# A hybrid decoder block on one core: norm 2's sums in halves, and five precomputed pieces placed differently around norm 2

## The chip, the core and the metric

The kernel runs on one core of one Trainium2 chip. The metric is the device time of one execution in microseconds (us). Before the change it took 804.24 us, the median of 3 runs (802.44 to 804.77).

## What is computed

One layer on 512 tokens of width 1024, all in float32. The reference, cut to what matters:

```python
h = rmsnorm(x, norm1_g)
z = h @ w_in + b_in
z_glu, z_rx, z_rg, z_ga, z_gb = split(z)
u   = silu(layernorm(causal_conv(glu(z_glu))))          # 31 taps
y_a = u @ conv_w_out + conv_b_out
y_b = (rg_lru(causal_conv(z_rx)) * gelu(z_rg)) @ lru_w_out
m = sigmoid(z_ga) * y_a + sigmoid(z_gb) * y_b
x = x + m @ w_mix_out
h = rmsnorm(x, norm2_g)                                  # "norm 2"
x = x + (silu(h @ ffn_w1) * (h @ ffn_w3)) @ ffn_w2       # d_ff = 2816
return rmsnorm(x, norm_f_g)
```

## The kernel before

**Products.** Each float32 operand is split into a high part (rounded to the matmul's format) and a low part (the rest), and a product is three matmuls: high by high, high by low, low by high. A weight chunk (512 KB) is loaded by SyncE into one of 4 `raw` buffers, ScalarE casts its high part (`split_to`, line 128), and VectorE (GpSimd in the first part of the kernel) subtracts for the low part (line 124) into one of 5 `hl` buffers. `emit_chunk` does this; the chunks have a fixed order and are asked for a few ahead.

**Seven products instead of eight.** Three large products (w_mix_out, most of ffn_w1/ffn_w3, ffn_w2) are cut into 2 x 2 blocks and made with seven block products, which needs sums of blocks on both sides. On the weights' side, the sums of ffn_w1, ffn_w3 and ffn_w2 are made piece by piece: `piece_load` brings two halves of 256 KB into one of 3 `wsums` buffers, `piece_sums` does four operations of 128 x 256 on GpSimd or VectorE (lines 124 and 375), and `piece_store` writes the 512 KB result to DRAM (line 379), from where it is later loaded as a chunk (`raw_ft`, `raw_ot`). Most pieces are made on GpSimd early in the kernel. The last four of ffn_w1/ffn_w3 and the first of ffn_w2 (`fwso` in the trace) are made around norm 2 by `mix_end`; the other pieces of ffn_w2 follow on VectorE in `out_step`.

**Around norm 2.** `mix_end` finishes the product with w_mix_out. Tokens are handled in two halves of 256 (tiles 0, 1 and tiles 2, 3). For each half the row sums of squares are made by ScalarE (lines 514 and 520), the rows scaled by VectorE (`xs`, line 1056), transposed by TensorE (line 538), and split into `h2h`, `h2l` by ScalarE and VectorE (lines 541 and 542). TensorE, ScalarE and VectorE follow the written order there. While the second half is prepared, TensorE multiplies the first half with the first four weight chunks f1_0, f3_0, f1_1, f3_1 (line 498); then it does the second half of these, the chunks f1_2 to f3_3 with all tokens, and from then on pairs of tiles by seven products (`ffn_seven`, line 1189), beginning with pair 2. Pair k uses the chunks fb11, fb20, fb21 (straight from the weights), ft00, ft01, ft10, ft11 (from the stored sums).

**On the activations' side** of `ffn_seven`, `f_inputs` needs the sum h2h + h2l of all eight row blocks: before, GpSimd makes these as eight operations of 128 x 512 (`hf`, line 1148) once norm 2 is wholly done. VectorE then makes four sums of 128 x 256 for each of four pairs (`hs`) and splits them (`hs_0h`, `hs_0l`, `hs_1h`, `hs_1l`).

**What orders the work.** Outside the written stretches a scheduler places the instructions; `tc.issue_after(x)` keeps an instruction behind instruction x. All transfers but a few stand in SyncE's queue, which issues them in its order: a transfer that waits (for a buffer or for a sum to be stored) holds all behind it. GpSimd, VectorE and ScalarE also run in order.

Of the kernel before, what the change touches and what calls it, by code (L numbers as in the profile page):

```python
# [8 lines left out]
F32 = mybir.dt.float32  # L9
F32R = mybir.dt.float32r  # L10
AF = mybir.ActivationFunctionType
ALU = mybir.AluOpType
# [14 lines left out]
ND = D // P  # L27
# [26 lines left out]
F_MIX, OUT_MIX, LATE_LAG = 4, 1, 8  # L54
# [37 lines left out]
def tile_block(ctx, tc, a, out):  # L92
    nc = tc.nc
# [8 lines left out]
    def tiles(tag, bufs):  # L102
        p_ = pool(tag, bufs)
        return lambda name, dtype=F32: p_.tile([P, T], dtype, tag=tag, name=name)

    longt, shortt = tiles("long", SLOTS), tiles("short", SHORT)

    def pairt(name, dtype=F32R):

        return longt(f"{name}h", dtype), longt(f"{name}l", dtype)  # L110
# [7 lines left out]
    vec, act, pe, pool_e = nc.vector, nc.scalar, nc.tensor, nc.gpsimd  # L118


    newest = {}

    def sub(eng, o, x, y):
        return eng.tensor_tensor(out=o, in0=x, in1=y, op=ALU.subtract)  # L124
# [9 lines left out]
    def split(name, full, eng, p_=None, copy=act.copy):  # L134
        p_ = p_ or pairt(name)
        return split_to(*p_, full, eng, copy)
# [40 lines left out]
    def emit_to(n):  # L177
        while emitted[0] < min(len(chunks), n):
            emit_chunk()
# [170 lines left out]
    def f_piece(k, i, c):  # L350

        four = (w1, w3)[i].rearrange("p (h k) n -> p h k n", h=2)
        halves = [four[:, h, c : c + 2, 2 * k * P : 2 * (k + 1) * P] for h in range(2)]
        return f"{k}_{i}_{c}", halves, f_sums[k][:, i, :, c * 256 : c * 256 + T]

    def o_piece(k, c):
        four = outq.w.rearrange("p (k h) (e n) -> p h k e n", h=2, e=2)
        cs = slice(256 * c, 256 * c + 256)
        return f"o{k}_{c}", [four[:, h, k, :, cs] for h in range(2)], outq.all_sums[k][:, :, cs]

    def piece_load(name, halves):
        raw = wsums.tile([P, 1024], F32, tag="wsum", name=f"fws{name}")
        for h, src in enumerate(halves):
            nc.sync.dma_start(raw[:, h * T : h * T + T].rearrange("p (e n) -> p e n", e=2), src)
        return raw

    def piece_sums(raw, dest, eng):
        if dest.shape[1] == 2:
            of = raw.rearrange("p (h k e n) -> p h e k n", h=2, k=2, e=2)
        else:  # L370
            of = raw.rearrange("p (h e n) -> p h e n", h=2, e=2)
        q11, q12, q21, q22 = (of[:, h, e] for h in range(2) for e in range(2))
        sub(eng, q22, q22, q12)
        sub(eng, q12, q12, q11)
        eng.tensor_tensor(out=q11, in0=q22, in1=q11, op=ALU.add)  # L375
        sub(eng, q21, q21, q11)

    def piece_store(raw, dest):
        nc.sync.dma_start(dest, raw.rearrange("p (m n) -> p m n", m=dest.shape[1]))
# [43 lines left out]
    x2_kept = [[dram.tile([P, T], F32, tag=f"x2k{t}{h}", name=f"x2k{t}{h}") for h in range(2)] for t in range(NT)]  # L423
# [8 lines left out]
    for name, n in ROWS:  # L432
# [4 lines left out]
        while done < n:  # L437
            m = min(n - done, P - row_at(at + done)[1])
# [70 lines left out]
    def rstd_begin(half, junk):  # L509

        i = n_stats[0]
        n_stats[0] += 1
        ss, r = stats[:, i, :2], stats[:, i, 2:3]
        act.activation(junk, half, AF.Square, accum_out=ss[:, 0:1])
        vec.tensor_scalar(out=ss[:, 0:1], in0=ss[:, 0:1], scalar1=1.0 / D, scalar2=EPS, op0=ALU.mult, op1=ALU.add)
        return ss, r

    def rstd_end(begun, half, junk):
        ss, r = begun
        act.activation(junk, half, AF.Square, accum_out=ss[:, 1:2])  # L520
        act.activation(r, ss[:, 1:2], AF.Sqrt, scale=1.0 / D, bias=ss[:, 0:1])
        vec.reciprocal(r, r)
        return r
# [222 lines left out]
    behind = [None, None]  # L746
# [114 lines left out]
    f_todo = [f_piece(k, i, c) for k in SEVEN for i in range(2) for c in (0, 2)]  # L861
    out_todo = [o_piece(k, c) for k in range(KF) for c in range(2)]
# [37 lines left out]
    LO, HI = HALVES  # L900
# [124 lines left out]
    x2 = [[longt(f"x2{t}{h}") for h in range(2)] for t in range(NT)]  # L1025
# [3 lines left out]
    h2p = [pairt(f"h2{c}") for c in range(ND)]  # L1029
    xs = []  # L1030

    def mix_end(second, plus, r1, r2, r7, third):
        todo = f_todo[-F_MIX:] + [out_todo.pop(0) for _ in range(OUT_MIX)]
        made = []

        def begin(behind=None):

            name, halves, dest = todo.pop(0)
            with tc.issue_after(behind or newest["any"]):
                made.append((piece_load(name, halves), dest))  # L1040
            piece_sums(*made[-1], pool_e)

        def store(behind=None):
            with tc.issue_after(behind or newest["any"]):
                piece_store(*made.pop(0))

        for _ in range(2):
            begin()
        sc = [[longt(f"xs{t}{h}") for h in range(2)] for t in range(NT)]
        xs.extend(sc)  # L1050
        begun = [rstd_begin(x2[t][0], sc[t][0]) for t in range(2)]

        def scaled(t, h):
            r = rstd_end(begun[t], x2[t][h], sc[t][h])
            for i in range(2):
                vec.tensor_scalar(out=sc[t][i], in0=x2[t][i], scalar1=r, scalar2=None, op0=ALU.mult)
                newest["kept"] = nc.sync.dma_start(x2_kept[t][i][:, :], x2[t][i]).ins


        with tc.manual_schedule(engines={ET.PE, ET.Activation, ET.DVE}):  # L1060
            second()
            plus(0, 1, r1[0])
            plus(0, 1, r2[0])
            plus(2, 1, r1[0])
            plus(1, 1, r1[1])
            plus(1, 1, r2[1])
            plus(3, 1, r1[1])
            for t in range(2):
                scaled(t, 1)
            begin(newest["kept"])  # L1070
            store(newest["kept"])

            for i in range(2):
                third(i, range(2))
            for q in range(2):
                turn_half("th", xs, "norm2_g", h2p, 0, [bank, bank2], range(4 * q, 4 * q + 4))
                for i in range(2):
                    third(i, [2 + q])
            begin()
            store()  # L1080
            for i in range(2):
                plus(2 + i, 1, r7[i])
                plus(2 + i, 0, r7[i])
            begun.extend(rstd_begin(x2[t][1], sc[t][1]) for t in (2, 3))
            emit_to(emitted[0] + 1)
            begin()
            for i in range(2):
                plus(2 + i, 0, r1[i])
            for t in (2, 3):
                scaled(t, 0)  # L1090
        while made:
            store()
        assert not todo

    m7.run(x2, lambda k: None, mix_end)


# [3 lines left out]
    def out_step(k):  # L1101


        if out_at[1]:
            with tc.issue_after(newest["any"]):
                piece_store(*out_at[1])
        if out_at[0]:
            with tc.issue_after(newest["now"]):
                piece_sums(*out_at[0], vec)
        out_at[1], out_at[0] = out_at[0], None  # L1110
        if out_quota.get(k, 0):
            out_quota[k] -= 1
            name, halves, dest = out_todo.pop(0)
            with tc.issue_after(newest["any"]):
                out_at[0] = piece_load(name, halves), dest
# [27 lines left out]

    def f_inputs():
        for k in range(4):
            a1, a2 = [longt(f"hf{c}") for c in (k, k + 4)]
            for v, c in ((a1, k), (a2, k + 4)):
                pool_e.tensor_tensor(out=v, in0=h2p[c][0].bitcast(F32), in1=h2p[c][1].bitcast(F32), op=ALU.add)
            g = [longt(f"hs{k}_{i}") for i in range(2)]
            s1, s2, s3, s4 = (v[:, cs] for v in g for cs in HALVES)  # L1150
            add(s1, a1[:, HI], a2[:, HI])
            sub(vec, s2, s1, a1[:, LO])
            sub(vec, s3, a1[:, LO], a1[:, HI])
            sub(vec, s4, a2[:, LO], s2)
            s12, s34 = [split(f"hs{k}_{i}", v, vec) for i, v in enumerate(g)]
            for n, p_, cs in (
                ("a11", h2p[k], LO), ("a12", h2p[k + 4], LO), ("a22", h2p[k + 4], HI),
                ("s1", s12, LO), ("s2", s12, HI), ("s3", s34, LO), ("s4", s34, HI),
            ):
                f_in[n].append(tuple(v[:, cs] for v in p_))  # L1160

    with tc.issue_after(turned):
        f_inputs()


    WHERE = {
# [80 lines left out]
    x2 = [[longt(f"x2b{t}{h}") for h in range(2)] for t in range(NT)]  # L1247
# [99 lines left out]
```

## Time and profile before

| | us |
|---|---|
| median of 3 runs | 804.24 |
| the profiled execution | 804.67 |
| its span, first to last instruction | 802.9 |
| TensorE busy | 791.2 |
| VectorE busy | 689.3 |
| ScalarE busy | 465.1 |
| GpSimd busy | 282.2 |

The mean TensorE clock granted is 0.999 of full speed. In the profile PE is TensorE (PEld its weight loads), DVE is VectorE, ACT is ScalarE, POOL is GpSimd and SPq is SyncE's queue. A row of a timeline gives the start and the duration in us, the engine, the line, the operation, output <- inputs, the shape, and in brackets the idle time before it and what ended that. Several equal operations in a row are merged (xN) and their joint duration given. Buffer numbers are left out of names, so that all `hl_f` chunks, for example, share one name; which is which follows from their order.

### The profile page before, as it was taken

What the parts mean: (1) busy time and instruction counts of PE and PEld (TensorE: products, weight loads), DVE (VectorE), ACT (ScalarE), POOL (GpSimd) and SP (SyncE); (2) the same over time, 40 slices, a digit from 0 to 9 for tenths busy, and PEclk for the clock granted to TensorE, in tenths of its full rate; (3) what the DMA queues carried; (4) which work ended last, traced back from release to release, by engine and by line L of the source; (5) the groups of instructions that cost most, each with busy time, mean ns of one, the idle gap of its engine ahead of it and who ended that gap; (6) DMA issues with size and microseconds to landing.
All of it is one profiled execution on the core that took longest, in us unless ns stands there. A gap on an engine that the chain in (4) does not pass through costs nothing.

```text
span 802.9 us, 12487 instructions
## 1 busy us (share of the span) xinstructions
PE 791.2 (99%) x4398; PEld 692.7 (86%) x4398; DVE 689.3 (86%) x1092; ACT 465.1 (58%) x666; POOL 282.2 (35%) x239
## 2 busy tenths in 40 slices
PE   8999999999999999999999999999999999999996
PEld 8988888888888888888888898899999999988885
DVE  5799999998999997776898868977778778999956
ACT  7446788766589655653336454444445445656753
POOL 2576678756878976112230365000000000000000
PEclk9999999999999999999999999999999999999999
DMA  7646565666676775578979768599889889878652
GB/s 221 188 125 178 164 193 168 205 198 175 196 215 207 238 242 160 171 238 268 301 250 306 233 217 262 159 312 298 288 287 302 275 283 305 272 225 282 202 171 105
DMA packets 188561, 182.35 MB, mean 227 GB/s; under 512 B 13671, under 2 KB 153363, under 8 KB 188499
## 3 DMA queue, kind: packets, MB, share of 16 engines
q1 hardware_dynamic: 188355, 181.30, 72.3%
q8 instruction: 34, 0.56, 0.3%
q14 instruction: 28, 0.23, 0.1%
q10 hardware_dynamic: 144, 0.26, 0.1%
HBM read 141.81 MB, written 36.70 MB: 222 GB/s over the span
## 4 chain that ended last, share of the span: by engine, by line
PE 85%; DVE 6%; DMA 5%; ACT 2%; issue 1%; SPq 1%; ACTq 0%; DVEq 0%
PE z L498 35%; PE fr L1189 15%; PE or L950 13%; PE yb L498 7%; PE ya L498 5%; PE mxr L950 5%; DMA raw_fb<-in_ffn_w_dram 3%; PE g L819 3%; PE f L498 2%; DVE hl_fb L124 1%; ACT hl_fb L128 1%; DVE fwso L124 1%; DMA raw_f<-in_ffn_w_dram 1%; DMA x<-in_x_dram 1%; DMA ot<-fwso 1%
## 5 line engine op out<-in xcount | busy, mean ns | idle before, releaser
L692 DVE SCALAR_TENSOR_TENSOR cv<-u,par,cv 128x511 f32<-128x511 f32 (+17 forms) x240 | 162.7, 728 | 1.1 <-ACT cv L689 0.9
L124 POOL TENSOR_TENSOR hl_in<-raw_in,hl_in 128x1024 fp32r<-128x1024 f32 x51 | 123.2, 2421 | 70.0 <-ACT hl_in L128 56.9
L124 POOL TENSOR_TENSOR fws<-fws 128x256 f32<-128x256 f32 x108 | 90.1, 838 | 125.8 <-DMA fws<-in_ffn_w_dram 120.9
L124 DVE TENSOR_TENSOR hl_fb<-raw_fb,hl_fb 128x1024 fp32r<-128x1024 f32 x27 | 34.1, 1263 | 29.1 <-ACT hl_fb L128 28.9
L1189 PE MATMUL fr<-hs_0h,hl_ft 128*128 128x256 f32 x288 | 53.8, 285 | 2.4 <-DVE hl_ft L124 1.6
L128 ACT CAST hl_in<-raw_in 128x1024 fp32r<-128x1024 f32 x51 | 53.1, 1042 | 1.1 <-issue 1.0
L128 ACT CAST hl_fb<-raw_fb 128x1024 fp32r<-128x1024 f32 x27 | 28.3, 1049 | 39.2 <-DMA raw_fb<-in_ffn_w_dram 34.0
L1189 PEld LDWEIGHTS fr<-hs_0h,hl_ft 128*128 128x128 f32 x288 | 45.5, 192 | 3.4 <-DVE hl_ft L124 1.8
L124 DVE TENSOR_TENSOR hl_ft<-raw_ft,hl_ft 128x1024 fp32r<-128x1024 f32 x36 | 43.8, 1218 | 4.7 <-ACT hl_ft L128 4.7
L498 PE MATMUL z<-h10h,hl_in 128*128 128x512 f32 (+1 forms) x110 | 41.4, 378 | 0.0
L498 PE MATMUL z<-h11h,hl_in 128*128 128x512 f32 (+1 forms) x110 | 41.1, 376 | 0.0
L498 PE MATMUL z<-h16h,hl_in 128*128 128x512 f32 (+1 forms) x110 | 41.1, 376 | 0.0
L498 PE MATMUL z<-h14h,hl_in 128*128 128x512 f32 (+1 forms) x110 | 41.1, 376 | 0.0
L498 PE MATMUL z<-h17h,hl_in 128*128 128x512 f32 (+1 forms) x110 | 41.1, 375 | 0.0
L498 PE MATMUL z<-h15h,hl_in 128*128 128x512 f32 (+1 forms) x110 | 41.1, 375 | 0.0
L498 PE MATMUL z<-h13h,hl_in 128*128 128x512 f32 (+1 forms) x110 | 41.1, 375 | 0.0
L498 PE MATMUL z<-h12h,hl_in 128*128 128x512 f32 (+1 forms) x110 | 41.1, 375 | 0.0
L1189 PE MATMUL fr<-hs_0l,hl_ft 128*128 128x256 f32 x144 | 40.7, 283 | 0.0
L1197 ACT ACTIVATE c<-c 128x256 f32<-128x256 f32 x27 | 11.3, 418 | 47.5 <-DVE c L899 47.4
L128 ACT CAST hl_ft<-raw_ft 128x1024 fp32r<-128x1024 f32 x36 | 36.8, 1042 | 2.8 <-DMA raw_ft<-fs 2.8
L128 ACT CAST hl_ob<-raw_ob 128x1024 fp32r<-128x1024 f32 (+1 forms) x23 | 23.4, 1016 | 21.3 <-PE or L950 13.4
L375 POOL TENSOR_TENSOR fws<-fws 128x256 f32<-128x256 f32 x36 | 28.9, 806 | 2.5
(940 smaller groups left out, 2618.5 us busy)
## 6 DMA issues: line engine op xcount, KB each, us to landing
raw_in<-in_w_in_dram SPq DMA_DIRECT2D x52, 512.0 KB
fws<-in_ffn_w_dram SPq DMA_DIRECT2D x72, 256.0 KB
fs<-fws SPq DMA_DIRECT2D x36, 512.0 KB
raw_ft<-fs SPq DMA_DIRECT2D x36, 512.0 KB
fwso<-in_ffn_w_dram SPq DMA_DIRECT2D x44, 256.0 KB
ot<-fwso SPq DMA_DIRECT2D x22, 512.0 KB
raw_fb<-in_ffn_w_dram SPq DMA_DIRECT2D x18, 512.0 KB
raw_ob<-in_ffn_w_dram SPq DMA_DIRECT2D x33, 256.0 KB
```

The lines of the kernel that those rows point to most:

```text
L124: return eng.tensor_tensor(out=o, in0=x, in1=y, op=ALU.subtract)
L128: copy(h, full)
L375: eng.tensor_tensor(out=q11, in0=q22, in1=q11, op=ALU.add)
L498: pe.matmul(ps, l, r, start=i == 0, stop=i == n - 1)
L692: vec.scalar_tensor_tensor(out=acc[c][:, s:], in0=u[c][:, : T - s], scalar=dw(c, s), in1=acc[c][:, s:], op0=ALU.mult, op1=ALU.add)
L819: pe.matmul(ps, l, r, start=k == 0, stop=k == len(mms) - 1)
L950: pe.matmul(banks[i], l_[:, ts], r_, start=start and n == 0, stop=stop and n == 2, skip_group_check=again)
L1189: pe.matmul(ps[:, HALVES[i]], lw[:, c, :], rx_, start=not (again or i or c or m), stop=bool(i and c == 3 and m == 2), skip_group_check=True,)
L1197: act.activation(c[:, LO], c[:, LO], AF.Silu)
```

## The change

1. GpSimd's eight sums `hf` of 512 columns become sixteen of 256 columns. Those of the first half of tokens (LO) stand in `mix_end`, behind the first half of norm 2; those of the second half (HI) stay in `f_inputs`.
2. Of the five pieces around norm 2, the first three are loaded ahead together. The sums of two are made at once as before, those of the third behind the first halves (LO). The fourth and fifth are loaded behind norm 2's written stretch, and their sums stand behind the second halves (HI), in turns in the program's order.
3. The stores of the first three pieces stand at the end of `mix_end`, behind the newest load there; those of the fourth and fifth are given out by `out_step`, one each time that it is called, behind the newest load.

```diff
+    mix_made = []
+    mix_todo = f_todo[-F_MIX:] + [out_todo.pop(0) for _ in range(OUT_MIX)]
+    f_full = []
+    def full(dst, c, cs):
+        newest["full"] = pool_e.tensor_tensor(out=dst, in0=h2p[c][0][:, cs].bitcast(F32), in1=h2p[c][1][:, cs].bitcast(F32), op=ALU.add).ins
...
-        for _ in range(2):
-            begin()
+        for n in range(3):
+            name, halves, dest = mix_todo.pop(0)
+            with tc.issue_after(newest["any"]):
+                made.append((piece_load(name, halves), dest))
+            if n < 2:
+                piece_sums(*made[-1], pool_e)
...
-            begin(newest["kept"])
-            store(newest["kept"])
...
-            begin()
-            store()
+            for c in range(ND):
+                f_full.append(longt(f"hf{c}"))
+                full(f_full[c][:, LO], c, LO)
+            with tc.issue_after(newest["full"]):
+                piece_sums(*made[2], pool_e)
...
-            begin()
...
+        if mix_made:
+            with tc.issue_after(newest["any"]):
+                piece_store(*mix_made.pop(0))
...
-            a1, a2 = [longt(f"hf{c}") for c in (k, k + 4)]
-            for v, c in ((a1, k), (a2, k + 4)):
-                pool_e.tensor_tensor(out=v, in0=h2p[c][0].bitcast(F32), in1=h2p[c][1].bitcast(F32), op=ALU.add)
+            a1, a2 = f_full[k], f_full[k + 4]
+            full(a1[:, HI], k, HI)
+            full(a2[:, HI], k + 4, HI)
...
+    with tc.issue_after(newest["any"]):
+        for name, halves, dest in mix_todo:
+            mix_made.append((piece_load(name, halves), dest))
     with tc.issue_after(turned):
         f_inputs()
+    for m in mix_made:
+        with tc.issue_after(newest["full"]):
+            piece_sums(*m, pool_e)
```

In the program that results, TensorE's instructions stand in the same order as before. In SyncE's queue the stores of the first two pieces now stand ahead of the load of chunk f1_2, and the third piece's store ahead of the load of f3_3. Then come the load of fb11, the fourth piece's store, the load of a piece of ffn_w2, the load of fb20, the fifth piece's store, the load of another piece, and the load of fb21.

More of the change, by code (lines that the diff above doesn't have):

```diff
@@ L1030, in tile_block, with store @@
     xs = []
+    mix_made = []
[3 more added lines that the diff above has]
+        newest["full"] = pool_e.tensor_tensor(out=dst, in0=h2p[c][0][:, cs].bitcast(F32), in1=h2p[c][1][:, cs].bitcast(F32), op=ALU.add).ins
     def mix_end(second, plus, r1, r2, r7, third):
-        todo = f_todo[-F_MIX:] + [out_todo.pop(0) for _ in range(OUT_MIX)]
         made = []
-        def begin(behind=None):
-            name, halves, dest = todo.pop(0)
-            with tc.issue_after(behind or newest["any"]):
-                made.append((piece_load(name, halves), dest))
[L1041 to L1045, printed above, removed]
-        for _ in range(2):
-            begin()
+        def store():
+            with tc.issue_after(newest["any"]):
+                piece_store(*made.pop(0))
+        for n in range(3):
+            name, halves, dest = mix_todo.pop(0)
+            with tc.issue_after(newest["any"]):
+                made.append((piece_load(name, halves), dest))
+            if n < 2:
+                piece_sums(*made[-1], pool_e)
         sc = [[longt(f"xs{t}{h}") for h in range(2)] for t in range(NT)]
@@ L1056, in scaled @@
                 vec.tensor_scalar(out=sc[t][i], in0=x2[t][i], scalar1=r, scalar2=None, op0=ALU.mult)
-                newest["kept"] = nc.sync.dma_start(x2_kept[t][i][:, :], x2[t][i]).ins
+                nc.sync.dma_start(x2_kept[t][i][:, :], x2[t][i])
         with tc.manual_schedule(engines={ET.PE, ET.Activation, ET.DVE}):
@@ L1092, in mix_end @@
             store()
-        assert not todo
     m7.run(x2, lambda k: None, mix_end)
@@ L1160, in f_inputs @@
                 f_in[n].append(tuple(v[:, cs] for v in p_))
+    with tc.issue_after(newest["any"]):
+        for name, halves, dest in mix_todo:
+            mix_made.append((piece_load(name, halves), dest))
     with tc.issue_after(turned):
         f_inputs()
+    for m in mix_made:
+        with tc.issue_after(newest["full"]):
+            piece_sums(*m, pool_e)
     WHERE = {
```

## The prediction

> **What bounds the kernel now.** I read the page first, then the waits of TensorE, the matmuls around the one long wait, and the engine in front of it. Part 1 of the page:
>
> ```profile
> PE 791.2 (99%) x4398; PEld 692.7 (86%) x4398; DVE 689.3 (86%) x1092; ACT 465.1 (58%) x666; POOL 282.2 (35%) x239
> ```
>
> TensorE is busy for 791.2 of 802.9 us, and the diff gives it the same matmuls in the same order. So the change can only act where TensorE waits. All its waits behind norm 2 (us in total, times, longest):
>
> ```profile
> PE fr L1189 <- DVE hl_ft L124: 1.6, 1, 1.6
> ...
> PE fr L1189 <- ACT c L1203: 0.6, 2, 0.3
> PE f L498 <- ACT h20h L541: 0.3, 1, 0.3
> ```
>
> The third is the turn of the second half of tokens (transpose, ScalarE, matmul); nothing in it is edited. The first two make 2.2 us: the most that the change can give, since it touches nothing else that TensorE waits for. The rows of TensorE in time (start, duration) place the long one:
>
> ```profile
> 470.12 0.60 PE L538 MATMUL th<-ident,xs 128*128 128x128 f32 x4
> ...
> 484.65 0.40 PE L498 MATMUL f<-h20l,hl_f 128*128 128x512 f32 x1
> ...
> 516.40 0.28 PE L1189 MATMUL fr<-hs_0l,hl_ft 128*128 128x256 f32 x1
> 518.25 0.50 PE L1189 MATMUL fr<-hs_0h,hl_ft 128*128 128x256 f32 x2 [1.57 <-DVE hl_ft L124]
> ```
>
> At 516.40 TensorE needs the low part of chunk ft01 of pair 2. VectorE makes it in program order, and these are its rows:
>
> ```profile
> 467.09 1.65 DVE L1056 TENSOR_SCALAR xs<-x,stats 128x512 f32<-128x512 f32 x2
> ...
> 476.32 0.48 DVE L542 SCALAR_TENSOR_TENSOR h27l<-th,par,h27h 128x256 fp32r<-128x256 f32 x1
> 476.72 1.41 DVE L124 TENSOR_TENSOR hl_f<-raw_f,hl_f 128x1024 fp32r<-128x1024 f32 x1
> 478.49 1.88 DVE L124 TENSOR_TENSOR hl_f<-raw_f,hl_f 128x1024 fp32r<-128x1024 f32 x1 [0.36 <-ACT hl_f L128]
> ...
> 481.34 1.28 DVE L124 TENSOR_TENSOR hl_f<-raw_f,hl_f 128x1024 fp32r<-128x1024 f32 x1 [0.18 <-ACT hl_f L128]
> 485.74 1.62 DVE L124 TENSOR_TENSOR hl_f<-raw_f,hl_f 128x1024 fp32r<-128x1024 f32 x1 [3.13 <-ACT hl_f L128]
> 487.28 0.41 DVE L1122 TENSOR_TENSOR ou<-si,f 128x256 f32<-128x256 f32 x1
> ...
> 488.72 2.31 DVE L124 TENSOR_TENSOR hl_fb<-raw_fb,hl_fb 128x1024 fp32r<-128x1024 f32 x1
> 490.95 1.77 DVE L124 TENSOR_TENSOR ous0l<-ou,ous0h 128x512 fp32r<-128x512 f32 x1
> ...
> 497.44 0.68 DVE L124 TENSOR_TENSOR hs_1l<-hs,hs_1h 128x512 fp32r<-128x512 f32 x1
> ...
> 500.76 1.22 DVE L124 TENSOR_TENSOR hl_fb<-raw_fb,hl_fb 128x1024 fp32r<-128x1024 f32 x1 [0.25 <-ACT hl_fb L128]
> ...
> 516.98 2.35 DVE L124 TENSOR_TENSOR hl_ft<-raw_ft,hl_ft 128x1024 fp32r<-128x1024 f32 x2
> ```
>
> VectorE reaches the wanted split only at 516.98, done near 518.1. Between 485.74 and 516.98 it hardly pauses, so its backlog is set at 485.74. Two things made it: a pause of 3.13 us before 485.74, and two splits that took 2.31 and 1.77 us where an equal shape takes 1.22 (500.76) and 0.68 (497.44). For the pause I follow ScalarE, SyncE's queue and the chain of waits:
>
> ```profile
> 461.40 1.98 ACT L128 CAST hl_f<-raw_f 128x1024 fp32r<-128x1024 f32 x2
> 464.33 0.63 ACT L520 ACTIVATE xs<-x 128x512 f32<-128x512 f32 x1 [0.94 <-DVE x L899]
> ...
> 484.66 1.05 ACT L128 CAST hl_f<-raw_f 128x1024 fp32r<-128x1024 f32 x1 [1.97 <-DMA raw_f<-in_ffn_w_dram]
> ```
>
> ```profile
> 453.30 0.42 SPq L153 DMA_DIRECT2D raw_f<-in_ffn_w_dram  x1
> ...
> 468.48 0.37 SPq L379 DMA_DIRECT2D fs<-fws  x1
> ...
> 477.08 0.60 SPq L379 DMA_DIRECT2D ot<-fwso  x1
> 477.74 1.61 SPq L1057 DMA_DIRECT2D x2k<-x  x2
> 479.39 0.65 SPq L153 DMA_DIRECT2D raw_f<-in_ffn_w_dram  x1
> ...
> 481.75 1.59 SPq L364 DMA_DIRECT2D fwso<-in_ffn_w_dram  x2
> 483.44 0.55 SPq L153 DMA_DIRECT2D raw_fb<-in_ffn_w_dram  x1
> ```
>
> ```profile
> 479.39 5.24 DMA raw_f<-in_ffn_w_dram
> ...
> 518.12 4.48 DMA ot<-fwso
> ...
> 562.90 7.03 DMA raw_fb<-in_ffn_w_dram
> ```
>
> The load of chunk f3_3 stood in SyncE's queue behind the store of the fifth piece (477.08), which waited for GpSimd. It was issued at 479.39, took 5.24 us, and ScalarE cast it at 484.66. GpSimd's rows:
>
> ```profile
> 447.02 1.82 POOL L375 TENSOR_TENSOR fws<-fws 128x256 f32<-128x256 f32 x1
> ...
> 452.08 0.74 POOL L124 TENSOR_TENSOR fws<-fws 128x256 f32<-128x256 f32 x1
> 464.96 1.74 POOL L124 TENSOR_TENSOR fws<-fws 128x256 f32<-128x256 f32 x2 [12.15 <-DMA fws<-in_ffn_w_dram]
> ...
> 477.01 2.28 POOL L1148 TENSOR_TENSOR hf<-h20h,h20l 128x512 f32<-128x512 f32 x1
> ...
> 483.73 1.29 POOL L1148 TENSOR_TENSOR hf<-h25h,h25l 128x512 f32<-128x512 f32 x1
> ```
>
> A sum over 256 columns takes 0.74 us, or 1.82 beside a large split of VectorE; one over 512 takes 1.29, or 2.28. So a blocked sum loses about 1.0 to 1.1 us.
>
> **The change part by part.**
>
> *First halves.* Eight sums of 256 columns follow norm 2's first half, 8 x 0.74 = 5.9 us, inside the 12.15 us that GpSimd idled before 464.96: hidden. The third piece is loaded with the first two, so its four sums follow at once, 4 x 0.74 plus one block of 1.08: done near 466. No engine waits there that waited for nothing before, except SyncE (second rival). If that cover went, GpSimd would reach the second halves later, and VectorE asks for those only behind the split of 490.95.
>
> *The load of f3_3* now has the third piece's store ahead of it: issued near 466 instead of 479.39. The 3.13 us pause goes. What is late next is TensorE: VectorE's product ou needs the first two tiles, whose last matmul ends where the next tile starts, 484.65, say 485.0 with its tail. Before, ou stood at 487.28: **2.3 us won** on VectorE.
>
> *Second halves and the two late pieces.* The second halves follow h27l (476.32 + 0.48); with a last one blocked by the split of 476.72, GpSimd is free near 478.9. Then come eight sums, of pieces four and five in turn; piece four is whole after the seventh. Seven x 0.74 = 5.2 us, plus three blocks of 1.08 by the splits like those of 478.49, 481.34 and 485.74, gives 487.3. Bounds: no block at all and the halves done at 477.5, 482.7; every sum at 1.82, 490.2 from 477.5 and 491.6 from 478.9. I take 487.3, because a block needs an overlap and there are three large splits. GpSimd then leaves VectorE alone from about 488 instead of 492, so the 1.09 + 1.09 us excess of the two splits mostly goes.
>
> By the Trainium skill, page "SBUF — State Buffer", section "SBUF: two separate sides", GpSimd and a VectorE instruction with two SBUF inputs take one port pair by an exclusive lock, and the other "fully blocks". The rows agree: 2.31 against 1.22 us, 1.82 against 0.74. By that rule alone every small VectorE sum would be a possible block as well, and piece four would be whole between 487.3 and the upper bound; it speaks against moving sums into this stretch.
>
> *SyncE's queue* is the price. Behind piece four's store now stand, in order, the loads of an output piece (1.59 us) and of chunk fb20, then the store of piece five, loads of the next output piece (which wait for piece four's buffer) and fb21. So fb20 is issued at 487.3 + 0.4 + 1.6 = 489.3, not at 483.44. It lands 5.24 us later, 494.5 (4.48 to 7.03 in the chain's rows: 493.8 to 496.3); cast 1.05, split 1.22, then hs_1l 0.68: 497.4. Before, VectorE ended hs_1l near 498.1. With everything loaded, VectorE would have been there at 498.1 - 2.3 - 2.2 = 493.6. So **the late load gives back 3.8 of 4.5 us**, and 0.7 to 0.8 are left. Chunk fb21: piece four's store lands 4.48 after 487.3, two loads of 1.6, so it is issued at 493.4, lands 498.6, is split by 501 at the latest; before, that split ended at 502.0. It adds nothing.
>
> *The rest of VectorE's queue* to ft01 holds the same instructions in a slightly other order, with GpSimd silent in both kernels: it moves by the same 0.8. The split ends at 517.3 instead of 518.1, and of the 1.57 us wait about 0.8 stays. The two waits for c (0.6 together) follow loads that themselves moved by 0.8, as TensorE did: they stay.
>
> *Sum.* 1.57 - 0.8 = 0.8 us saved. The profiled execution took 804.67 us for a span of 802.9; it lies 0.4 above the median of 804.24. From the median: 804.24 - 0.8 = **803.4 us**.
>
> **The rivals.**
>
> *The gain is whole.* If GpSimd is hardly blocked (piece four at 482.7 to 486), fb20 lands 1.3 to 4.6 us sooner, VectorE is at least 2.1 us ahead, and the 1.57 go, with up to 0.6 of the waits for c: 2.2 us, **802.0**. For it speaks that 464.96 shows 0.87 a sum beside VectorE; against it, that five large splits fall into 476.7 to 488.
>
> *The new wait takes all (the other side).* Mechanism: SyncE stands before piece four's store, and VectorE waits for fb20. It decides at 487.3 + 0.8 = 488.1: every microsecond that GpSimd ends later lengthens TensorE's wait by the same. At 491.6, every sum blocked, ft01 is done 3.5 us later than before: **807.7**. For it: 477.01, where sums ran at 2.28 in a row; against: VectorE has no pieces that dense between 480 and 485.
>
> *No net change.* GpSimd at about 488, or one landing 0.8 us slower (7.03 stands in the chain): **804.2**, a new wait in the place of the old.
>
> *Norm 2 itself late.* The load of f1_2 now queues behind the stores of the first two pieces, whose sums end at 452.08 + 0.74, and one copy of x2: issued near 454, where the load of 453.30 stood. ScalarE casts it in the pair at 461.40, ahead of the squares of 464.33. VectorE ends xs at 468.74 and TensorE wants it at 470.12: 1.4 us of slack. A landing after 464.7, 10.7 us after issue against 7.03 at most above, would cost one for one; at 467, 2.3 us: **806.5**. Unlikely.
>
> That the change doesn't do what it says can be left out: the moved sums stand so in the program.
>
> **How the numbers follow.** Forecast (0.2 to 1.4 saved, 802.8 to 804.0) 0.40; whole gain 0.20; no net change 0.16; late fb20 0.18; norm 2 late 0.06. Runs of before spread over 802.44 to 804.77, so about 0.3%, 2.4 us, is what a measurement can tell from no change. Faster than 801.8 needs the whole gain and luck: 0.10. Slower than 806.65 needs the outer half of the two slow cases: 0.12. Within: 0.78. Range: 801.4 (whole gain and 0.6 of spread) to 806.6 (where at most one in ten is above).
>
> **What would show it.** Right: VectorE's pause before the fourth hl_f split gone, and a pause of two to four us before the second hl_fb instead, behind a load that SyncE issued right behind piece four's store near 487; TensorE's wait for hl_ft near 0.8. Wrong: GpSimd's eight late sums done before 485 and no pause at that split (whole gain), or ended after 489 with a longer wait for hl_ft; ScalarE's squares of the second half waiting for a cast.

## The result, and the profile after

The changed kernel takes 805.76 us (median of 22 runs, 804.79 to 808.77), the kernel before 804.12 us (22 runs in turns with it, 801.47 to 806.07). The ratio is 1.0025, with a 95% interval of 1.0016 to 1.0035: **slower** by 1.6 us by the medians and 2.0 by the ratio, where 0.8 us faster was forecast.

The profiled execution of after took 804.81 us, span 802.7 us, which is near the fastest of its runs; that of before took 804.67, which is above its median. So these two profiles, set side by side, show almost no difference; three more of each kernel stand below. TensorE's waits behind norm 2 in after (us in total, times, longest):

```profile
PE fr L1203 <- ACT c L1217: 1.3, 2, 1.0
PE fr L1203 <- DVE hl_ft L124: 1.2, 1, 1.2
...
PE f L498 <- ACT h20h L541: 0.3, 1, 0.3
```

The wait for chunk ft01 (hl_ft) went from 1.57 to 1.23, not to 0.8, and the waits for c (ScalarE's copy of a finished block product, which has to be made before TensorE adds the next product to it) went from 0.6 to 1.3. TensorE's rows in time, each wait with the matmul ahead of it and the one behind it where they are used below:

```profile
470.90 0.97 PE L498 MATMUL f<-h20h,hl_f 128*128 128x256 f32 x5 [0.35 <-ACT h20h L541]
...
514.56 0.28 PE L1203 MATMUL fr<-hs_1h,hl_fb 128*128 128x256 f32 x1
515.15 0.39 PE L1203 MATMUL fr<-hs_0h,hl_ft 128*128 128x256 f32 x1 [0.31 <-ACT c L1217]
515.37 0.28 PE L1203 MATMUL fr<-hs_0l,hl_ft 128*128 128x256 f32 x1
...
518.31 0.50 PE L1203 MATMUL fr<-hs_0h,hl_ft 128*128 128x256 f32 x2 [1.23 <-DVE hl_ft L124]
...
538.03 0.39 PE L1203 MATMUL fr<-hs_0h,hl_ft 128*128 128x256 f32 x1 [0.99 <-ACT c L1217]
```

VectorE's rows that answer to those of before (start, duration):

```profile
483.49 1.73 DVE L124 TENSOR_TENSOR hl_f<-raw_f,hl_f 128x1024 fp32r<-128x1024 f32 x1 [0.65 <-ACT hl_f L128]
485.15 0.41 DVE L1130 TENSOR_TENSOR ou<-si,f 128x256 f32<-128x256 f32 x1
...
491.70 0.68 DVE L124 TENSOR_TENSOR hs_0l<-hs,hs_0h 128x512 fp32r<-128x512 f32 x1
496.36 1.23 DVE L124 TENSOR_TENSOR hl_fb<-raw_fb,hl_fb 128x1024 fp32r<-128x1024 f32 x1 [3.98 <-ACT hl_fb L128]
497.50 0.68 DVE L124 TENSOR_TENSOR hs_1l<-hs,hs_1h 128x512 fp32r<-128x512 f32 x1
...
517.04 2.35 DVE L124 TENSOR_TENSOR hl_ft<-raw_ft,hl_ft 128x1024 fp32r<-128x1024 f32 x2
```

The old pause (3.13 us before 485.74) is gone, and ou stands at 485.15 where 485.0 was forecast. A new pause of 3.98 us stands before the split of fb20, where two to four were forecast. Yet hs_1l ends at 498.18, not at 497.4: that is where it ended before, and from there VectorE runs as late as before (517.04 against 516.98). GpSimd's seventh late sum, which makes piece four whole, SyncE's queue and ScalarE's cast of fb20 show the chain:

```profile
485.79 0.75 POOL L124 TENSOR_TENSOR fws<-fws 128x256 f32<-128x256 f32 x1
```

```profile
465.55 0.42 SPq L153 DMA_DIRECT2D raw_f<-in_ffn_w_dram  x1
...
478.14 0.93 SPq L339 DMA_DIRECT2D raw_fb<-in_ffn_w_dram  x2
486.56 0.37 SPq L379 DMA_DIRECT2D fs<-fws  x1
487.02 1.35 SPq L364 DMA_DIRECT2D fwso<-in_ffn_w_dram  x2
488.46 0.60 SPq L153 DMA_DIRECT2D raw_fb<-in_ffn_w_dram  x1
489.15 0.60 SPq L379 DMA_DIRECT2D ot<-fwso  x1
489.84 1.70 SPq L364 DMA_DIRECT2D fwso<-in_ffn_w_dram  x2
491.63 1.49 SPq L153 DMA_DIRECT2D raw_fb<-in_ffn_w_dram  x1
```

```profile
495.28 1.05 ACT L128 CAST hl_fb<-raw_fb 128x1024 fp32r<-128x1024 f32 x1 [3.85 <-DMA raw_fb<-in_ffn_w_dram]
```

Piece four is whole at 486.54 (forecast 487.3) and SyncE stands from 479.07 to 486.56 before its store. The load of fb20, issued at 488.46, lands at 495.28: 6.8 us, not 5.24. The stretches of the DMA queue show what it left with (length, clock, busy share of the 16 DMA engines, GB/s):

```profile
484.00:488.00 4.00, 1.00 0.14 52
488.00:490.00 2.00, 1.00 0.89 263
...
492.00:494.00 2.00, 1.00 1.06 365
494.00:496.00 2.00, 1.00 1.08 380
```

While SyncE waited, the DMA engines were all but idle; then two stores, four loads of pieces and fb21 came out together with fb20 and shared the engines with it. In the other three executions of after the same load took 7.0, 6.3 and 6.9 us. That the crowd stretched it is argued from these rows and not tested: before, f3_3's 5.24 us fell into engines that were about as busy (0.84 to 1.07 between 478 and 484).

### The profile page after: what moved, and what is told of

It reads as the page before. It is cut to its first block, busy times and chain, and to the rows that moved or that the text cites. A ratio compares the mean times of both kernels' runs of the same rounds, so it can differ in the third digit from the quotient of the medians.

```text
span 802.7 us, 12502 instructions
## 1 busy us (share of the span) xinstructions
PE 791.2 (99%) x4398; PEld 692.9 (86%) x4398; DVE 686.9 (86%) x1092; ACT 465.1 (58%) x666; POOL 281.6 (35%) x247
## 4 chain that ended last, share of the span: by engine, by line
PE 88%; DVE 5%; DMA 3%; ACT 1%; issue 1%; SPq 0%; DVEq 0%; ACTq 0%
PE z L498 35%; PE fr L1203 17%; PE or L950 13%; PE yb L498 7%; PE ya L498 5%; PE mxr L950 5%; PE g L819 3%; PE f L498 3%; DMA raw_fb<-in_ffn_w_dram 1%; DMA ot<-fwso 1%; DVE fwso L124 1%; DVE hl_ft L124 1%; DVE hl_fb L124 1%; DMA x<-in_x_dram 1%; PE th L538 0%
```

## The experiments

The theory: the load of fb20, held in SyncE's queue behind GpSimd's late sums, eats VectorE's lead. The rivals: that ScalarE's and VectorE's new order behind pair 2 costs by itself; that GpSimd's sums cost through the port that they share with VectorE; that the difference is noise of the kernel's start.

One table for all. "Split" is the start of VectorE's split of ft01, counted from the row of TensorE's first matmul behind the second turn (470.90 in after, the first row above); "behind" is the time from that row to the end of the span. In the kernel with the sums ahead (E2), where TensorE waits for nothing there, it wants ft01 45.45 us behind that row; a split needs 1.27 us from its start to the waiting matmul (517.04 to 518.31), so the split must start by 44.2.

| kernel | median us (runs) | ratio to before, 95% | split | behind |
|---|---|---|---|---|
| before, four profiles | 804.12 (22) | | 45.9, 44.3, 45.3, 46.2 | 331.8, 330.1, 331.3, 331.7 |
| after, four profiles | 805.76 (22) | 1.0025 (1.0016 to 1.0035) | 46.1, 46.4, 45.6, 46.2 | 331.8, 332.6, 331.7, 332.5 |
| E2 sums ahead | 801.15 (12) | 0.9973 (0.9958 to 0.9988) | 40.8 | 328.2 |
| E3 halves alone | 801.11 (12) | 0.9970 (0.9956 to 0.9985) | 41.9 | 328.2 |
| E4 pieces alone | 807.63 (7) | 1.0053 (1.0031 to 1.0074) | 42.8 | 333.9 |
| E6 stores later | 802.30 (12) | 0.9979 (0.9964 to 0.9993) | 42.2 | 329.2 |
| E7 in turn | 802.93 (12) | 0.9984 (0.9973 to 0.9995) | 42.7 | 330.0 |
| E8 load early | 804.15 (12) | 0.9997 (0.9985 to 1.0008) | 45.1 | 331.6 |

The medians follow the last column: from E2 to the mean of before (331.2) it grows by 3.0, and so do they.

**E1, the changed kernel again.**

> The changed kernel again, unedited, for a second profile. First theory (the held load): the profile shows VectorE's pause of 3 to 5 us ahead of the second hl_fb split and TensorE's wait for hl_ft at 0.8 to 2 us again, 804.8 to 807. Rival (the gain is there, and something unrelated, such as the start of the kernel or the clock, moves the time from run to run): the waits behind norm 2 differ by over 1 us between the two profiles, or the time differs where these waits are the same.

Measured: 805.79 us (12 runs), ratio 1.0024 (1.0008 to 1.0040). The wait for hl_ft is 1.22 and VectorE's pause 4.19; the waits for c are 1.7. The first theory's line held. TensorE's waits at the start differ between the two profiles (2.0 us against 0.5), but its row behind the second turn comes only 0.2 us later; 0.8 of the 1.0 us between the two spans lies behind that row, where the waits for c are longer.

**E2, the late sums ahead of the second halves.** Only GpSimd's order changes.

```diff
...
     with tc.issue_after(newest["any"]):
         for name, halves, dest in mix_todo:
             mix_made.append((piece_load(name, halves), dest))
-    with tc.issue_after(turned):
-        f_inputs()
     for m in mix_made:
-        with tc.issue_after(newest["full"]):
+        with tc.issue_after(newest["sums"]):
             piece_sums(*m, pool_e)
+    with tc.issue_after(turned):
+        f_inputs()
```

> The changed kernel with one thing moved: GpSimd makes the sums of pieces four and five ahead of the second halves (HI) and not behind them, so that their stores hold nothing up in SyncE's queue. All other engines keep the order of the changed kernel. First theory (the held load of fb20 is what eats the lead): fb20's load is issued near 481 to 484, not 488.5, VectorE's pause ahead of its split goes, TensorE's wait for hl_ft at 518 goes from 1.2 to 0, and the time falls by 1.2 to 2.2 us, to about 803.7 at the median, below the kernel before or equal to it. Rival (VectorE's and ScalarE's order behind pair 2, the same in both, makes the waits): the time stays within 0.5 us of the changed kernel, with 2 us or more of waits behind norm 2. Second rival (GpSimd and VectorE share a port, and the sums now meet norm 2's second half): TensorE waits for h2 near 470 to 480 and the time rises.

Measured: 801.15 us, by the medians 4.6 below the changed kernel and 2.9 below the kernel before, more than was expected. Behind norm 2 TensorE's only wait is the turn. SyncE issues fb20 at 481.33, the DMA engines are busy at 1.04 from 480 to 484, where the share was 0.35 in after, and VectorE has no pause ahead of fb20's split and, behind GpSimd's last sum, no stretched one (SyncE, a stretch, GpSimd's last sum, VectorE):

```profile
481.33 0.62 SPq L153 DMA_DIRECT2D raw_fb<-in_ffn_w_dram  x1
```

```profile
480.00:484.00 4.00, 1.00 1.04 318
```

```profile
478.50 1.72 POOL L1038 TENSOR_TENSOR hf<-h27h,h27l 128x256 f32<-128x256 f32 x1
```

```profile
483.42 1.23 DVE L124 TENSOR_TENSOR hl_f<-raw_f,hl_f 128x1024 fp32r<-128x1024 f32 x1 [1.09 <-ACT hl_f L128]
...
511.63 2.35 DVE L124 TENSOR_TENSOR hl_ft<-raw_ft,hl_ft 128x1024 fp32r<-128x1024 f32 x2
```

The split of ft01 starts 5.4 us sooner. The order of VectorE and ScalarE is the changed kernel's (as it is in E3, E6 and E7), and its waits for c are gone too: the order alone costs nothing. What this run leaves open is which of the two, the queue or the port, did it, since the late sums are out of VectorE's way as well.

**E3, the halves alone**, in the kernel before; the five pieces stay, only the third piece's sums stand behind the first halves.

```diff
...
-            begin(newest["kept"])
+            begin(newest["kept"], False)
+            third_piece = made[-1]
...
+            for c in range(ND):
+                f_full.append(longt(f"hf{c}"))
+                full(f_full[c][:, LO], c, LO)
+            with tc.issue_after(newest["full"]):
+                piece_sums(*third_piece, pool_e)
             begin()
...
-            for v, c in ((a1, k), (a2, k + 4)):
-                pool_e.tensor_tensor(out=v, in0=h2p[c][0].bitcast(F32), in1=h2p[c][1].bitcast(F32), op=ALU.add)
+            full(a1[:, HI], k, HI)
+            full(a2[:, HI], k + 4, HI)
```

> The kernel before with part one of the change alone: norm 2's sums in halves of tokens, the first halves at once; the five pieces' loads and stores stay where they were, with the third piece's sums behind the first halves. First theory: no load behind norm 2 is held longer than before, f3_3's load still waits for the stores (the 3 us pause of VectorE stays), the second halves are done 5 us sooner than the whole sums were, and the time is that of the kernel before within 0.8 us, 803.3 to 804.5. Rival (the halves themselves cost, by more operations on the shared port): 805 to 806, as the changed kernel.

Measured: 801.11 us. Neither line held: it was expected to change nothing, and it takes 3.0 us off the median. GpSimd is done at 485.45, not at 492, and leaves VectorE alone from there:

```profile
484.71 0.74 POOL L1035 TENSOR_TENSOR hf<-h27h,h27l 128x256 f32<-128x256 f32 x1
```

```profile
487.57 1.22 DVE L124 TENSOR_TENSOR hl_fb<-raw_fb,hl_fb 128x1024 fp32r<-128x1024 f32 x1
488.70 0.69 DVE L124 TENSOR_TENSOR ous0l<-ou,ous0h 128x512 fp32r<-128x512 f32 x1
```

Before, the last two took 2.31 and 1.77. Of the change's parts it is the early half of the sums that pays, and TensorE waits for nothing more behind the turn: the waits for c are gone with the one at ft01.

**E4, the pieces alone**: the changed kernel with whole sums behind norm 2, and the third piece's sums made at once.

```diff
-            if n < 2:
-                piece_sums(*made[-1], pool_e)
+            piece_sums(*made[-1], pool_e)
...
-            for c in range(ND):
-                f_full.append(longt(f"hf{c}"))
-                full(f_full[c][:, LO], c, LO)
-            with tc.issue_after(newest["full"]):
-                piece_sums(*made[2], pool_e)
...
-            full(a1[:, HI], k, HI)
-            full(a2[:, HI], k + 4, HI)
+            for v, c in ((a1, k), (a2, k + 4)):
+                newest["full"] = pool_e.tensor_tensor(out=v, in0=h2p[c][0].bitcast(F32), in1=h2p[c][1].bitcast(F32), op=ALU.add).ins
```

> The changed kernel without its halves: norm 2's sums are made whole (128 x 512) once norm 2 is done, the third piece's sums at once, pieces four and five behind the whole sums. In this program the stores of pieces four and five stand behind the loads of fb20, fb21 and the ft chunks, so that no load waits for them. First theory: f3_3 early and fb20 not held, VectorE has the lead of 2 us or more at 517, TensorE's wait for hl_ft is gone, 802 to 803.5, unless the whole sums come too late for hs (done after 491: then VectorE waits for hf, and one for one TensorE). Rival (the placing of the pieces moves traffic into pair 2 and costs by itself): 805 to 806.

Measured: 807.63 us. No load of pair 2 waits for the late stores here, and it is the slowest kernel, slower than both theories had it. GpSimd's late sums run until 496.6, and beside them VectorE's small sums take twice as long as the first one behind them:

```profile
494.20 0.95 DVE L899 TENSOR_TENSOR hs<-hf,hf 128x256 f32<-128x256 f32 x1
...
496.94 0.43 DVE L124 TENSOR_TENSOR hs<-hf,hs 128x256 f32<-128x256 f32 x1
```

So GpSimd's sums hold VectorE up here, but that this costs time is not shown: the split of ft01 still starts in time (42.8), and TensorE doesn't wait there. Its waits are others: 2.79 us for c in pair 3, where ScalarE stood behind the cast of an ft chunk that landed late, with the clock at half behind it (last section), then 0.27 and 0.44 for hl_ft. Why that chunk was late stays open; the late stores and the loads in SyncE's queue stand in another order here too. So E4 is no clean test of either theory.

**E6 and E7, the queue and its dose.** E6 keeps GpSimd's order of the changed kernel and gives the late stores out one call later, so that fb20's load stands ahead of the first. E7 keeps SyncE's order and makes the sums of piece four before those of piece five, so that piece four is whole after four late sums, not seven.

```diff
+    calls = []
+
     def out_step(k):
-        if mix_made:
+        calls.append(k)
+        if mix_made and len(calls) > 1:
```

```diff
+    newest["sums"] = newest["full"]
     for m in mix_made:
-        with tc.issue_after(newest["full"]):
+        with tc.issue_after(newest["sums"]):
             piece_sums(*m, pool_e)
```

(In E2 and E7 `piece_sums` notes its last operation in `newest["sums"]`.)

> The changed kernel with the stores of pieces four and five given out one call of out_step later: the load of fb20 stands ahead of the fourth piece's store, that of fb21 ahead of the fifth's. GpSimd's order is that of the changed kernel, so its late sums still run beside VectorE's splits. First theory (the load held in SyncE's queue is the cost): fb20 is issued near 481.5, VectorE's pause of 4 us ahead of its split goes, the wait for hl_ft goes, 801 to 802. Rival (GpSimd's late sums beside VectorE are the cost, through the shared port, and sums_ahead won by ending them 8 us sooner): 804 or more, with VectorE's splits at 1.7 and the wait for hl_ft still there.

> The changed kernel with the late sums of piece four wholly ahead of those of piece five, and not in turns: the same eight sums on GpSimd, the same queue on SyncE, but piece four is whole after four sums, not seven: near 483.5 and not 486.5. First theory, by its dose: fb20's load is issued 3 us sooner, VectorE gains 3 us, which is more than the 1.2 us that TensorE waits: the wait for hl_ft goes to 0 to 0.3, the time to 801 to 802.3. Rival (the port): the splits stay blocked by as many sums, and the time stays at 805 to 806.

Measured: 802.30 and 802.93 us, 3.5 and 2.8 below the changed kernel, in the direction of the first theory and 0.3 and 0.6 above its ranges. E6 (SyncE, then VectorE): fb20 is issued at 481.40, there is no pause, and the split still runs at 1.76 beside GpSimd.

```profile
481.40 0.59 SPq L153 DMA_DIRECT2D raw_fb<-in_ffn_w_dram  x1
```

```profile
487.71 1.76 DVE L124 TENSOR_TENSOR hl_fb<-raw_fb,hl_fb 128x1024 fp32r<-128x1024 f32 x1
...
492.68 0.68 DVE L124 TENSOR_TENSOR hs_0l<-hs,hs_0h 128x512 fp32r<-128x512 f32 x1
493.39 1.23 DVE L124 TENSOR_TENSOR hl_fb<-raw_fb,hl_fb 128x1024 fp32r<-128x1024 f32 x1
...
514.08 2.36 DVE L124 TENSOR_TENSOR hl_ft<-raw_ft,hl_ft 128x1024 fp32r<-128x1024 f32 x2
```

E7: the fourth piece's store goes at 484.35, fb20's load at 486.24.

```profile
484.35 0.37 SPq L379 DMA_DIRECT2D fs<-fws  x1
...
486.24 0.60 SPq L153 DMA_DIRECT2D raw_fb<-in_ffn_w_dram  x1
```

With the queue free and GpSimd's order as in after, the split starts 3.9 us sooner (42.2 against 46.1); with the sums out of VectorE's way as well (E2), 1.4 us more. In VectorE's lead, taken in this order, that is the size of the queue and of GpSimd's late sums. In the time, what stays of E6's and E7's distance to E2 are waits for c, the longest in pair 4 (0.4 and 1.15 us), whose cause stays open, and 0.3 us outside the span (below).

**E8, the early load alone**: the kernel before, with the fifth piece's store no longer ahead of f3_3's load.

```diff
...
-        while made:
+        while len(made) > 1:
             store()
-        assert not todo
+        mix_made.extend(made)
...
     def out_step(k):
+        if mix_made:
+            with tc.issue_after(newest["any"]):
+                piece_store(*mix_made.pop(0))
```

> The kernel before with one thing moved: the fifth piece's store is given out by out_step, behind the load of fb11, and no longer stands ahead of f3_3's load. Nothing is done in halves and no piece is moved on GpSimd. The prediction's step on f3_3 says that this load alone wins 2.3 us on VectorE, more than the 1.6 us of the wait for hl_ft: that wait goes, and the time falls by 1.6 to 2.9 us, to 801.2 to 802.5. Rival (VectorE is held by GpSimd's whole sums up to 485 anyway, so an earlier split is only a longer split): the time falls by less than 0.8 us, 803.3 to 804.1.

Measured: 804.15 us, no different from before. The load is issued at 472.40, 7 us sooner, the pause falls to 0.44, and the second hl_fb split stands where it stood before (495.74 against 495.70). VectorE's rows, and GpSimd's last:

```profile
486.22 0.41 DVE L1127 TENSOR_TENSOR ou<-si,f 128x256 f32<-128x256 f32 x1
...
487.66 2.31 DVE L124 TENSOR_TENSOR hl_fb<-raw_fb,hl_fb 128x1024 fp32r<-128x1024 f32 x1
489.89 1.78 DVE L124 TENSOR_TENSOR ous0l<-ou,ous0h 128x512 fp32r<-128x512 f32 x1
491.59 1.51 DVE L124 TENSOR_TENSOR os1p<-os,os1p 128x256 fp32r<-128x256 f32 x1
...
495.74 1.22 DVE L124 TENSOR_TENSOR hl_fb<-raw_fb,hl_fb 128x1024 fp32r<-128x1024 f32 x1
```

```profile
491.08 1.74 POOL L1153 TENSOR_TENSOR hf<-h27h,h27l 128x512 f32<-128x512 f32 x1
```

The rival held. The time that VectorE won it spent beside GpSimd's whole sums, which end at 492.8: 1.09, 1.09 and 1.10 us more on three rows.

**E5 and E9 to E12, the two kernels again.** The medians differ by 1.6 us and the first two profiles by 0.1.

> The kernel before again, unedited, for a second profile. If its waits behind norm 2 are the same in every run, the starts of TensorE's matmuls lag those of the kernel with the sums ahead by 3.3 to 3.9 us behind norm 2, as in the first profile. Rival (the first profile was one of its slow executions, which would explain why the two profiles show no difference and the medians 1.7 us): a lag of 2 to 3 us, with a wait for hl_ft of 1.2 or less.

> A third profile of the kernel before. It is to tell whether TensorE's wait at ft01 of pair 2, 1.57 us in the first profile and none in the second, comes and goes from run to run. Theory: VectorE's split of ft01 stands between 515 and 517, near the 516.5 at which TensorE wants it, so the wait is between 0 and 1.6. Rival: it is 1.4 or more in most executions, and the second profile was the exception.

> A third profile of the changed kernel. Theory: since fb20's load waits for GpSimd's eight sums behind norm 2, which vary little, VectorE's pause ahead of the second hl_fb split is 3.3 us or more and the wait for hl_ft 1.1 us or more in every execution. Rival: both vary as they do in the kernel before, and this profile shows a wait under 0.6.

> A fourth profile of the kernel before, for the same question: a wait for hl_ft between 0 and 1.6, by the theory not the same as in the first.

> A fourth profile of the changed kernel, for the same question: a wait for hl_ft of 1.1 us or more again, by the theory.

Measured: 804.23 us for E5 (12 runs; ratio 0.9998, 0.9984 to 1.0012), and 804.82, 806.17, 805.24 and 805.60 for the single runs (one more run of before beside them took 802.11). E5's lag behind E2 is 1.9 us, just below the 2 to 3 of its rival. The idle row at ft01 in before is 1.57 us, none, 0.92 and 1.87; in after 1.23, 1.22, 1.23 and 1.23. The waits for c in total: 0.6, 0.8, 0.4 and 0 in before, 1.3, 1.7, 1.5 and 1.7 in after; E5 and E9 have one wait more each (0.29 for hl_ft, 0.66 for hl_fb). The theory held in the main: after, VectorE is late every time; before, it stands at the edge (44.3 to 46.2, where 44.2 is in time) and the wait comes and goes. E11's 1.87 lies above the 1.6 that was expected.

What moves VectorE before is GpSimd. The end of its last whole sum in the first execution, the same in E5, and the split of ft01 in E5:

```profile
489.91 2.27 POOL L1148 TENSOR_TENSOR hf<-h27h,h27l 128x512 f32<-128x512 f32 x1
```

```profile
488.18 2.27 POOL L1148 TENSOR_TENSOR hf<-h27h,h27l 128x512 f32<-128x512 f32 x1
```

```profile
515.26 2.35 DVE L124 TENSOR_TENSOR hl_ft<-raw_ft,hl_ft 128x1024 fp32r<-128x1024 f32 x2
```

In all four executions the split starts 24.8 us behind that end (492.18 to 516.98; 490.45 to 515.26; 492.22 to 517.03; 493.08 to 517.87), while the pause ahead of f3_3's split is 3.13, 0.61, 1.39 and 3.48 us. GpSimd's last chain of sums, in turn, starts when a piece's load lands (473.87, 472.18, 473.93 and 474.77).

From the first matmul behind the turn to the end, before takes 331.2 us on average and after 332.15, 0.9 more. The start is the same (471.35 and 471.34 on average). A further 0.3 us lies outside the span: 1.8 us in the four executions of before, 2.1 in the four of after (2.1 in E6 and E7 too, 1.8 in E2, E3, E4 and E8); nothing shown here explains it. That is 1.2 of the 1.6 that the medians differ by; four profiles each, which scatter by 0.4 to 0.8, can't place the rest.

## Why the prediction went wrong, step by step

*First halves, hidden in GpSimd's idle time:* right. The last of them ends at 461.04.

*The load of f3_3, "2.3 us won on VectorE":* the rows came as forecast (issued 465.55, ou at 485.15), but the reason, that the pause of 3.13 us had cost VectorE these 2.3, was **wrong**. E8 has that load early and wins nothing, because VectorE is held until GpSimd's sums end; in the four executions of before the pause varies by 2.9 us, and the split of ft01 follows GpSimd's end and not the pause. Without the halves the early load is worth 0; with the halves alone (E3), and that load at 477.70, where E5 has it too (477.69), TensorE waits for nothing more behind the turn.

*Second halves and the two late pieces:* the size was right (486.54 against 487.3).

*SyncE's queue, "the late load gives back 3.8 of 4.5 us":* the mechanism was right and **a term of it was mis-sized**. The load was issued 0.8 us sooner than forecast and took 6.8 us, not 5.24: the duration was that of f3_3's load, while this one left with everything that had queued up behind the same store. hs_1l ended at 498.18, not 497.4, so the whole lead was gone; that was the rival *no net change*, "one landing 0.8 us slower". E6 measures both sides, by the split of ft01: a lead of 3.7 us over the first execution of before (45.9 to 42.2), and 3.9 given back. The time is above that rival's 804.2; the next step has a part of the rest.

*The rest of VectorE's queue; "the two waits for c ... stay":* **wrong**. They grew from 0.6 to 1.3. In pair 3 VectorE's sum for c stands behind a split in the new order (at 536.37, behind that of 534.56; before at 533.59, ahead of it); ScalarE's silu waits for the sum (537.08, 1.66 us), and the copy that TensorE wants stands behind the silu (537.41). E2 has that order and no such wait, so it takes the order and the lateness together: VectorE's 5.4 us in E2 hide what costs 1.3 in after.

*"2.2 us: the most that the change can give":* **too small**. From the turn to the end E2 and E3 take 328.2 us and the first execution of before 331.8: 3.6 us lie in TensorE's waits, whose idle rows made 2.2. The three waits with a row cost 1.83, 0.56 and 0.58 by the starts of the matmuls, and two more leave no row and cost 0.40 (at 557.84) and 0.30 (at 659.49) (last section). Over its four executions before takes 331.2, so 3.0 us were to be had on average, and E2 and E3 have them: 2.9 and 3.0 by the medians, 2.2 and 2.4 (within 1.0 to 3.5) by the ratios.

*The sum itself* was taken off one execution, in which the wait at ft01 was 1.57 us. In three others there was none, 0.92 and 1.87. What the change did was to put a steady lateness in the place of one that comes and goes, and a profile of one execution can't show that a wait is only sometimes there.

*By the Trainium skill*, page "SBUF — State Buffer", section "SBUF: two separate sides", whoever starts first gets the shared port pair for the whole instruction. The sum counted blocks for large splits alone and left this rule as the dearer case. The rows of E4 (0.95 against 0.43) and E8 (1.51 for a sum of 0.41) agree with the page: a small sum of VectorE waits out an instruction of GpSimd as well.

The version that beats both kernels is the change with the late sums ahead of the second halves (801.15 us), or the halves alone (801.11); between these two the runs tell no difference.

## What to carry to other kernels

Moving work behind a deadline in an in-order queue of transfers delays not that work but every load behind it, and when the queue opens they all leave at once; so put the store that waits behind the loads that don't, or finish its input while the engine is idle. Before an early load is counted as a gain, look whether the engine that uses it is held by something else until later. And where a wait of about a microsecond decides, take several profiles of the kernel before: ask in how many of its executions the wait is there.

## What the runs showed of the hardware that was not expected

A wait of TensorE costs more than its idle row. In after, the matmuls around the first wait for c start at 514.56, 515.15 and 515.37, where neighbours start 0.12 us apart: 0.81 instead of 0.24, so 0.57 lost for an idle row of 0.31. At 538.03 it is 1.25 for 0.99. So some 0.26 us come on top of each wait. Two things in the rows make it: a matmul's row lasts 0.28 us where the next starts 0.12 behind it, so the first 0.16 of a wait don't show as idle; and the first matmul behind a wait takes 0.22 to the next start, not 0.12. A short wait can therefore go unlisted: in the first execution of before the starts around 557.84 are 557.42, 557.84 and 558.06, so 0.40 is lost, and the idle time of 0.14 that is left has no entry.

Behind two long waits the granted clock fell to half. The wait of 1.87 us in E11 (the kernel before) is followed by these stretches (length, busy and matmuls, clock, DMA share, GB/s):

```profile
519.15 0.51 PE L1189 MATMUL fr<-hs_0h,hl_ft 128*128 128x256 f32 x2 [1.87 <-DVE hl_ft L124]
```

```profile
520.00:522.00 2.00, 2.00 (x15) 0.66 1.00 301
522.00:524.00 2.00, 2.00 (x11) 0.50 0.98 271
524.00:526.00 2.00, 2.00 (x18) 0.98 1.03 355
```

By the rows of the timeline the 18 matmuls from 520.56 to 524.21 took 3.65 us, where 0.12 apart they take 2.16: 1.5 us lost. E4 shows the same behind its wait of 2.79 us (0.64 and 0.51), while behind this stage's waits of 1.57 us and less the clock stayed at 1.00. That the waits did it is inferred from their place, and the length alone doesn't settle it: at the start of E10 waits of 1.06, 0.55 and 1.13 us, ended at 6.51, 8.32 and 10.63, were followed by 0.73 and 0.50. By the Trainium skill, page "TensorE: Matmul & The Clock Gate", section "HAM oscillation — how this bites in real kernels", the gap to avoid is one of more than about 3.4 us; in E11 the clock fell behind 1.87, in the one execution that shows such a wait, and the measurement decides.
